# HGRN2 readout on 32-column TensorE tiles, gates computed ahead of the backward direction, and 40 unread products a layer between HGRN2 and banded attention

## The chip, the cores and the metric

One core of a Trainium2 chip runs the whole program: a two-layer hybrid diffusion backbone. TensorE (PE) does the products and the transposes, VectorE (DVE) and ScalarE (ACT) the elementwise work, GpSimd (POOL) a little, and SyncE (SP) issues the DMAs. The metric is device time in microseconds (us) of one execution.

## The reference, cut to what matters

Each layer feeds the same normalised tokens (256 of context and 1024 latent) to four groups of heads: an S5 state space model, banded attention, HGRN2 and latent attention. HGRN2 has four heads with a state of 64 x 64, runs in both directions, and is computed in chunks of 32 tokens. With f the forget gate, q the query and v the value of a token, one head of one direction does

```
S_t = diag(f_t) S_(t-1) + (1 - f_t) v_t^T       # state, 64 keys x 64 values
y_t = q_t^T S_t                                 # readout
y   = rms_norm(y_fwd + y_bwd) * g * silu(gate)
```

In chunks, y of a token is the sum of an intra part (products of the 32 tokens of its own chunk, masked by a triangle) and an inter part (its decayed query times the state that enters the chunk). Latent tokens start from the last context state; in the last layer nothing is read out for context tokens.

## The kernel before

Features lie on the partitions and tokens on the free axis. The 1280 tokens come in blocks (0, 512), (512, 512) and (1024, 256); the last is the context. HGRN2 has two passes p = 0, 1 in each layer, and a pass holds two heads (64 partitions each). In a pass, `fm` computes a dense product of a block with 128 columns of the input projection (tiles `psfm`, 24 products of 128x512 or 128x256, three for each of eight slices of the features, lines L509 to L511) and hands the PSUM tile on. In this order a pass takes: the queries (`query`), the three forward units, the three backward units (`unit`, called with the direction and the block), and for each block the gate and the end (`finish`). Between these calls the S5 mixer and, in layer 0, the modulation columns (`mods`; tiles `modps`, `modt`) are written a step at a time.

One unit of a 512-token block goes through the engines like this. ACT makes a softplus of the dense tile (L568 to L570), DVE the log gates (L571, L572) and their sum in each chunk (a scan, L580). ACT expands the decay to 128x1024 (L590), makes the decayed query and key (L594, L595) and the key decayed to the chunk's end (L599). PE transposes that (L604), ACT copies it (L605), PE multiplies it with v for every chunk (L613, 64 records), ACT copies the four results (L614) into the state tile `hgkv`, in which value column v and chunk c stand at v * 17 + c, so that one DVE scan (L621) runs over all chunks. Then comes the readout: PE multiplies keys with queries of 128 tokens a head (L631), DVE copies through the triangle's mask into `hgatt`, zero outside the diagonal (L633), and PE sums the intra product (L640) and the inter products (L644) in one tile `hgop`. Here the state of a chunk is the stationary operand, 64 columns at a stride of 17 floats, and 32 tokens of queries are the moving one. ACT copies `hgop` to `hgy` for the forward direction (L647), DVE adds it for the backward one (L649).

`finish` copies the gate's dense tile, makes its silu (L350 to L354, L660), squares y (L662), multiplies the square with a matrix of ones (L664, tile `hgms`), takes the inverse root on ACT (L673, L674), and ends on DVE (L666, L667) with a DMA to DRAM. Its temporary tiles `hglg` are those of the units.

The order of each engine is made at build time by a scheduler that sees tile dependencies. PSUM gives `fm` three buffers, and five of another tag (`mx`) are shared by HGRN2, S5 and the modulation. After HGRN2 comes banded attention (tiles `sws`, `swP`, L788 on), in whose PSUM pool latent attention also starts.

Of the kernel before, what the change touches and what calls it, by code (L numbers as in the profile page):

```python
# [10 lines left out]
U8 = mybir.dt.uint8  # L11
# [524 lines left out]
class HGRN:  # L536
# [12 lines left out]
    def start(self, p):  # L549
        self.p = p  # L550
        self.q, self.y, self.prev = {}, {}, [None, None]
# [6 lines left out]
    def unit(self, d, b, z):  # L558
# [6 lines left out]
        vt = self.pool.tile([128, 4, 128], F32, name="hgv", bufs=1)[:, 0:m]  # L565
        nc.sync.dma_start(vt, self.vd[:, t0 // 128:t0 // 128 + m, p * 128:p * 128 + 128])
        lg, sp, lf, cum = self.new("lg", tn, 2), self.new("sp", tn, 2), self.new("lf", tn), self.new("cum", tn)
# [31 lines left out]
        nc.scalar.activation(out=sp, in_=sp, func=AF.Exp, scale=-1.0, bias=bias)  # L599

# [6 lines left out]
        for q in range(4):  # L607
            r = slice(32 * q, 32 * q + 32)
            ps = self.ps(f"kvp{q}")[:, 0:64 * m].rearrange("p (m v) -> p m v", v=64)
            for i in range(m):  # L610
                for h in range(2):
                    hs = slice(64 * h, 64 * h + 64)
                    nc.tensor.matmul(ps[hs, i], kt[r, i, hs], vt[r, i, hs], start=True, stop=True)  # L613
# [11 lines left out]
        ats = []  # L625
        for h in range(2):
            r = slice(64 * h, 64 * h + 64)
            ps = self.ps(f"at{h}")[:, 0:tn].rearrange("p (m t) -> p m t", t=128)
            for i in range(m):
                ts = slice(i * 128, i * 128 + 128)  # L630
                nc.tensor.matmul(ps[:, i], kp[r, ts], qd[r, ts], start=True, stop=True)  # L631
            at = g.hgatt[h][d][:, 0:m]
            V.copy_predicated(at, g.hgtri[:, d].unsqueeze(1).to_broadcast([128, m, 128]), ps)  # L633
            ats.append(at)
        op = self.ps("op")[:, 0:tn]
        heads = slice(0, 64), slice(64, 128)
        for i in range(m):
            cl = [c for c in range(4 * i, 4 * i + 4) if before[c] is not None]
            for r, at in zip(heads, ats):
                nc.tensor.matmul(op[r, i * 128:i * 128 + 128], vt[:, i, r], at[:, i], start=True, stop=not cl)  # L640
            for c in cl:
                ts = slice(c * HC, c * HC + HC)
                for r in heads:
                    nc.tensor.matmul(op[r, ts], before[c][r], qd[r, ts], start=False, stop=c == cl[-1])  # L644
        if d == 0:
            self.y[b] = self.pool.tile([128, tn], F32, name=f"hgy{b}", bufs=1)
            nc.scalar.copy(self.y[b], op)  # L647
        else:
            V.tensor_tensor(out=self.y[b], in0=self.y[b], in1=op, op=OP.add)  # L649

    def finish(self, b, gg, ng, dst):
# [1494 lines left out]
```

## Time and profile before

| what | value |
|---|---|
| time, median of 3 runs | 3580.84 us (3575.26 to 3581.83) |
| profiled execution, its own time | 3594.48 us |
| its span | 3592.4 us |
| PE busy | 3374.6 us, 94% of the span |
| DVE, ACT busy | 2242.0 us (62%), 1517.0 us (42%) |
| mean granted clock of TensorE | 0.925 |
| HGRN2 with S5, layer 0 and layer 1 | 285 to 682 us, 2245 to 2512 us |

The busy times are those of one profiled execution, and its time lies 13.6 us above the median of the runs. The two HGRN2 stretches are read off the first and the last of their instructions in the timeline. Matmuls are pipelined, so that the duration of one record in the timeline is longer than the time to the next record; where records repeat, the start of the next group tells the pace. [...]

### The profile page before, as it was taken

The page shows a single profiled execution, that of the slowest core. Times are in us where ns is not written, and L with a number is a line of the kernel's source. Part 1 is how long each engine was busy: PE and PEld are TensorE (multiplying, and loading weights), DVE is VectorE, ACT ScalarE, POOL GpSimd, SP SyncE. Part 2 cuts the span into 40 slices and gives each one's busy share as a digit, 9 for nine tenths or more (in the row PEclk, how much of TensorE's full clock was granted, in tenths as well). Part 3 has the DMA queues.
Part 4 walks back from the last instruction along what each step waited for, and adds up shares of the span by engine and source line. Part 5 has one row for each costly group of instructions (what it writes and reads, how often), then busy time and mean ns, then how long its engine had stood idle before and what let it go on. Part 6 is the DMA issues. An engine that isn't in the chain of part 4 may idle for free.

```text
span 3592.4 us, 49905 instructions
## 1 busy us (share of the span) xinstructions
PE 3374.6 (94%) x18452; PEld 2564.5 (71%) x18452; DVE 2242.0 (62%) x4615; ACT 1517.0 (42%) x2804; POOL 210.5 (6%) x165
## 2 busy tenths in 40 slices
PE   7999999899999899999999999898999989999898
PEld 4876766555457777888788887776554668888786
DVE  8764454446746988555487724655566576566676
ACT  4144334334544523333354524655344553333344
POOL 0000000002320000000000000000035100000000
PEclk9998887579999899999999999887699999999999
DMA  6434353312032333222544433222010423333733
GB/s 206 156 128 154 121 168 111 97 41 70 29 116 98 108 109 115 87 93 74 203 160 117 129 105 109 78 85 60 18 45 11 155 98 122 97 106 106 246 97 109
DMA packets 251860, 389.54 MB, mean 108 GB/s; under 512 B 41648, under 2 KB 125840, under 8 KB 250848
## 3 DMA queue, kind: packets, MB, share of 16 engines
q1 hardware_dynamic: 240208, 374.69, 32.2%
q0 software_dynamic: 2192, 8.23, 0.9%
q10 hardware_dynamic: 9216, 3.44, 0.4%
q8 instruction: 145, 2.38, 0.3%
q14 instruction: 99, 0.81, 0.1%
HBM read 283.42 MB, written 102.83 MB: 108 GB/s over the span
## 4 chain that ended last, share of the span: by engine, by line
PE 81%; DVE 10%; ACT 4%; DMA 3%; issue 1%; SPq 0%; ACTq 0%; DVEq 0%
PE fpd L510 4%; PE fpd L511 4%; PE fpd L509 4%; PE fpx L509 4%; PE fpx L510 4%; PE fpx L511 4%; PE psfm L509 3%; PE psfm L511 3%; PE psfm L510 3%; PE mlo L1044 3%; PE fpw L509 2%; PE fpw L511 2%; PE fpw L510 2%; PE hgop L644 2%; PE sws L790 2%; PE pso L509 2%
## 5 line engine op out<-in xcount | busy, mean ns | idle before, releaser
L509 PE MATMUL fpd<-bhr,dhr 128*128 128x512 f32 (+1 forms) x792 | 280.5, 368 | 17.9 <-ACT bhr L515 10.3
L510 PE MATMUL fpd<-blr,dhr 128*128 128x512 f32 (+1 forms) x792 | 291.6, 370 | 2.3 <-DVE blr L518 2.3
L511 PE MATMUL fpd<-bhr,dlr 128*128 128x512 f32 (+1 forms) x792 | 289.1, 367 | 0.0
L509 PE MATMUL psfm<-Hh,wfh 128*128 128x512 f32 (+1 forms) x704 | 269.8, 383 | 1.8 <-ACT hgq L556 1.2
L511 PE MATMUL psfm<-Hh,wfl 128*128 128x512 f32 (+1 forms) x704 | 265.9, 378 | 0.0
L510 PE MATMUL psfm<-Hl,wfh 128*128 128x512 f32 (+1 forms) x704 | 264.7, 376 | 0.0
L509 PE MATMUL fpx<-Th,fh 128*128 128x512 f32 x528 | 208.3, 394 | 25.2 <-ACT fh L515 22.9
L515 ACT CAST fh<-fs 128x512 fp32r<-128x512 f32 x176 | 108.8, 621 | 239.9 <-PE fpc L510 68.8
L510 PE MATMUL fpx<-Tl,fh 128*128 128x512 f32 x528 | 207.7, 393 | 1.8 <-DVE Tl L1290 1.8
L511 PE MATMUL fpx<-Th,fl 128*128 128x512 f32 x528 | 207.3, 393 | 0.0
L515 ACT CAST fh<-fq 128x512 fp32r<-128x512 f32 x160 | 99.1, 621 | 222.1 <-issue 93.5
L509 PEld LDWEIGHTS fpd<-bhr,dhr 128*128 128x128 f32 x792 | 147.4, 190 | 42.8 <-ACT bhr L515 18.3
L518 DVE TENSOR_TENSOR fl<-fq,fh 128x512 fp32r<-128x512 f32 x160 | 109.9, 688 | 106.6 <-ACT fh L515 106.6
L510 PEld LDWEIGHTS fpd<-blr,dhr 128*128 128x128 f32 x792 | 150.0, 189 | 30.6 <-DVE blr L518 5.4
L1014 DVE TENSOR_REDUCE mlmc<-mls 128x1 f32<-128x512 f32 (+1 forms) x200 | 114.3, 590 | 88.1 <-PE mls L1013 87.6
L511 PEld LDWEIGHTS fpd<-bhr,dlr 128*128 128x128 f32 x792 | 150.0, 189 | 24.1 <-issue 0.2
L509 PEld LDWEIGHTS psfm<-Hh,wfh 128*128 128x128 f32 x704 | 137.1, 195 | 36.0 <-issue 12.3
L511 PEld LDWEIGHTS psfm<-Hh,wfl 128*128 128x128 f32 x704 | 136.6, 194 | 29.4 <-issue 9.2
L510 PEld LDWEIGHTS psfm<-Hl,wfh 128*128 128x128 f32 x704 | 137.0, 195 | 26.6 <-issue 7.4
L1040 ACT ACTIVATE mlpt<-mlst 128x512 f32<-128x512 f32 (+1 forms) x168 | 97.5, 585 | 113.9 <-PE mlst L511 107.3
L1077 POOL TENSOR_TENSOR mlac<-mlac,mlpt 128x1024 f32<-128x1024 f32 x56 | 137.5, 2455 | 116.2 <-ACT mlpt L1040 115.5
L518 DVE TENSOR_TENSOR fl<-fs,fh 128x512 fp32r<-128x512 f32 x176 | 120.8, 688 | 29.0 <-ACT fh L515 26.5
(529 smaller groups left out, 8539.1 us busy)
## 6 DMA issues: line engine op xcount, KB each, us to landing
fq<-in_w_up SPq DMA_DIRECT2D x188, 256.0 KB, 2.6
btok<-gd SPq DMA_DIRECT2D x154, 256.0 KB, 2.8
modw<-in_w_mod SPq DMA_DIRECT2D x128, 256.0 KB, 3.7
gd<-fg SPq DMA_DIRECT2D x88, 256.0 KB, 2.1
gd<-fgt SPq DMA_DIRECT2D x66, 256.0 KB, 2.1
mw<-in_w_down SPq DMA_DIRECT2D x66, 256.0 KB, 4.5
mw<-in_w_mod SPq DMA_DIRECT2D x32, 512.0 KB, 6.1
wor<-in_w_out SPq DMA_DIRECT2D x32, 512.0 KB, 3.6
```

The lines of the kernel that those rows point to most:

```text
L509: nc.tensor.matmul(ps, wh, xh, start=first and i == 0, stop=False, skip_group_check=read)
L510: nc.tensor.matmul(ps, wh, xl, start=False, stop=False, skip_group_check=read)
L511: nc.tensor.matmul(ps, wl, xh, start=False, stop=last and i == n - 1, skip_group_check=read)
L515: i = g.nc.scalar.copy(hi, src)
L518: (eng or g.nc.vector).tensor_tensor(out=lo, in0=src, in1=hi.bitcast(F32), op=OP.subtract)
L644: nc.tensor.matmul(op[r, ts], before[c][r], qd[r, ts], start=False, stop=c == cl[-1])
L790: nc.tensor.matmul(out, q[r], kl[r, c0:c1], start=False, stop=stop)
L1014: V.tensor_reduce(out=mc[:, qb, j:j + 1], in_=s, axis=AX.X, op=OP.max)
L1040: nc.scalar.activation(out=pt, in_=ps, func=AF.Exp, scale=MLA_SCALE)
L1044: nc.tensor.matmul(po[c], vt[:, b, 64 * h:64 * h + 64], pt[:, e], start=first, stop=last)
L1077: (V if h == 3 and b > 5 else nc.gpsimd).tensor_tensor(out=acc, in0=acc if b > 1 else prev, in1=pt, op=OP.add)
```

## The change

It has four parts.

1. **Readout.** Keys times queries is done for a chunk of 32 tokens alone: 32 products of 32x32 a unit (new L608) instead of 8 of 128x128. It stands ahead of the transposes, and the masked copy (L612, now 128 columns a head) ahead of the state scan. The intra product is 32 products on 32x32 tiles (L645), the inter product 32 products (L650), in which the decayed query is the stationary operand (64 x 32) and the state of the chunk, 64 columns at a stride of 17 floats, the moving one. So y comes out with tokens on the partitions, in two tiles (one a head), and `finish` transposes it back on PE (L679, tile `hgyt`, four of 128x128 for a block of 512).
2. **Order.** A new `gate` (copy, sigmoid, product into `hgsg`) is called for all blocks before the backward direction, and `finish` of a block right behind its backward unit. The plan in which the input projection's weights are loaded follows.
3. **Buffers.** `hglg` has one buffer in place of two, `hgv` two in place of one, `hgatt` becomes two small tiles a direction, the mask of the scan is bfloat16.
4. **Unread products.** 40 bfloat16 products of 128x256 (L1815, tile `run`) are written ahead of banded attention; nothing reads them. The scheduler sets them between the instructions of the last unit.

```diff
-        lg, sp, lf, cum = self.new("lg", tn, 2), self.new("sp", tn, 2), self.new("lf", tn), self.new("cum", tn)
+        lg, sp, lf, cum = self.new("lg", tn), self.new("sp", tn, 2), self.new("lf", tn), self.new("cum", tn)
...
+            for i in range(m):
+                for c in range(4):
+                    ts = slice(i * 128 + c * HC, i * 128 + c * HC + HC)
+                    for r, ps in zip(heads, pss):
+                        nc.tensor.matmul(ps[32 * c:32 * c + 32, i], kp[r, ts], qd[r, ts], start=True, stop=True)
+            at = g.hgatt[d][self.count[d] % 2]
+            self.count[d] += 1
+            for h in range(2):
+                V.copy_predicated(at[:, h, 0:m], g.hgtri[:, d].unsqueeze(1).to_broadcast([128, m, HC]), pss[h])
...
-                nc.tensor.matmul(ps[:, i], kp[r, ts], qd[r, ts], start=True, stop=True)
...
-            for r, at in zip(heads, ats):
-                nc.tensor.matmul(op[r, i * 128:i * 128 + 128], vt[:, i, r], at[:, i], start=True, stop=not cl)
-            for c in cl:
-                ts = slice(c * HC, c * HC + HC)
-                for r in heads:
-                    nc.tensor.matmul(op[r, ts], before[c][r], qd[r, ts], start=False, stop=c == cl[-1])
+            for h, r in enumerate(heads):
+                for c in range(4):
+                    k = slice(32 * c, 32 * c + 32)
+                    nc.tensor.matmul(ops[h][k, i], at[k, h, i], vt[k, i, r], start=i == 0, stop=False)
+        for c in range(n):
+            if before[c] is not None:
+                k = slice(32 * (c % 4), 32 * (c % 4) + 32)
+                for h, r in enumerate(heads):
+                    nc.tensor.matmul(ops[h][k, c // 4], qd[r, c * HC:c * HC + HC], before[c][r], start=False, stop=c == end[c % 4])
...
+        yt = self.ps("yt")[:, 0:tn]
+        for i in range(0, tn, 128):
+            nc.tensor.transpose(yt[:, i:i + 128], y[:, i:i + 128], g.ident)
+        nc.scalar.activation(out=sq, in_=yt, func=AF.Square)
...
                     for b, t0, tn, ps in fm(4 * p + 3, last):
-                        hg.finish(b, ps, g.hgng[:, l:l + 1], ysc[p][l])
+                        hg.gate(b, ps)
                         next(s5, None)
+                    for b, t0, tn, ps in fm(4 * p + 1, order=(2, 1, 0)):
+                        hg.unit(1, b, ps)
+                        next(s5, None)
+                        if not last or t0 < TL:
+                            hg.finish(b, g.hgng[:, l:l + 1], ysc[p][l])
...
+            ps = mpp.tile([128, 512], F32, name="run", tag="mdp")
+            for _ in range(40):
+                nc.tensor.matmul(ps[:, 0:256], g.identb, g.swmask.rearrange("p a b -> p (a b)"), start=True, stop=True)
```

On ACT, the last two backward units of layer 0 stood like this before: the copies of one unit's state products (L614), then already the next unit's decay (L590), whose softplus lies further ahead, and at the end three `finish` calls in a row.

```order
L614 COPY hgkv<-hgkvp_5971 128x4x64
L590 ACTIVATE hgdec<-hgcum 128x64x16
L595 ACTIVATE hgkp<-hgsp 128x512
L599 ACTIVATE hgsp<-hgsp 128x512
L1136 COPY modr<-modps 128x256 x2
L605 COPY hgkt<-hgtp 128x512
L614 COPY hgkv<-hgkvp_6129 128x4x64
```

Now, at the same place (L626 is the copy of the state products, L680, L691 and L692 are the three ACT steps of `finish`, L568 the first step of the next unit):

```order
L626 COPY hgkv<-hgkvp_6587 128x4x64
L680 ACTIVATE hglg<-hgyt 128x512
L691 ACTIVATE hglg<-hgms,eps 128x512
L692 ACTIVATE hglg<-hglg 128x512
L568 ACTIVATE hglg<-psfm 128x512
L569 ACTIVATE hglg<-hglg 128x512
L570 ACTIVATE hglg<-hglg 128x512
L590 ACTIVATE hgdec<-hgcum 128x64x16
```

The next unit's softplus moved behind the whole `finish` of the unit ahead of it.

On PE, the end of HGRN2 in layer 1 stood like this before (the last dense product, the last of four groups of readout, the two `hgms` and the first two products of banded attention):

```order
L511 MATMUL psfm<-Hh_18818,wfl 128x512
L640 MATMUL hgop<-hgatt_20418,hgv 64x128
...
L644 MATMUL hgop<-hgqd,hgkv 64x32 x8
L664 MATMUL hgms<-hglg,ones_134 128x512 x2
L788 MATMUL sws<-swo_22864,swo_22870 128x256
L790 MATMUL sws<-swkl,swo_22870 128x256
```

Now the last dense product stands ahead of the key products of the last unit but one, and a whole unit with its `finish` follows between the `run` products:

```order
L511 MATMUL psfm<-Hh_19830,wfl 128x512
L608 MATMUL hgat_23436<-hgqd,hgkp 32x32
...
L617 MATMUL hgtp<-ident,hgsp 128x128 x4
...
L682 MATMUL hgms<-hglg,ones_134 128x512
L1815 LDWEIGHTS identb
L1815 MATMUL run<-swmask,identb 128x256
...
L679 MATMUL hgyt<-ident,hgy_22915 128x128 x4
L682 MATMUL hgms<-hglg,ones_134 128x512
L805 MATMUL sws<-swo_23896,swo_23902 128x256
```

The dense products that stood between the units of the last pass moved ahead of the last two backward units. In layer 1, 24 `run` products stand ahead of the last unit's key products and 16 between its steps; in layer 0, 13 stand ahead, 25 between and 2 behind.

## Rows read from the trace of the kernel before

**Rows 1.** The page: engines' busy time, TensorE's granted clock in 40 slices, last chain.

```profile
PE 3374.6 (94%) x18452; PEld 2564.5 (71%) x18452; DVE 2242.0 (62%) x4615; ACT 1517.0 (42%) x2804; POOL 210.5 (6%) x165
...
PEclk9998887579999899999999999887699999999999
...
PE 81%; DVE 10%; ACT 4%; DMA 3%; issue 1%; SPq 0%; ACTq 0%; DVEq 0%
```

**Rows 2.** Windows: start:end, length, busy (records) by engine, granted clock, DMA share, GB/s.

```profile
280.00:690.00 410.00, 370.32 (x3100) 265.30 (x3099) 200.05 (x402) 161.37 (x317) 8.02 (x24) 0.80 0.41 127
2240.00:2512.00 272.00, 238.16 (x2127) 189.80 (x2125) 168.96 (x315) 148.50 (x275) 8.23 (x24) 0.83 0.25 77
636.80:681.90 45.10, 34.34 (x291) 21.37 (x291) 14.04 (x22) 15.60 (x26) 0.21 (x1) 0.53 0.19 58
2495.60:2511.80 16.20, 9.76 (x85) 6.12 (x85) 6.20 (x9) 5.64 (x10) 0.00 (x0) 0.62 0.09 21
698.00:768.00 70.00, 70.00 (x252) 41.88 (x251) 29.73 (x80) 21.99 (x56) 1.76 (x3) 0.54 0.14 43
2512.00:2558.00 46.00, 42.02 (x131) 24.98 (x130) 23.37 (x51) 18.48 (x41) 1.58 (x1) 0.50 0.13 37
```

**Rows 3.** Groups by line on PE: records, busy us, mean ns, idle before.

```profile
L644 PE MATMUL hgop<-hgqd,hgkv 64*64 64x32 f32 x1136 | 79.2, 295 | 0.0
L640 PE MATMUL hgop<-hgatt,hgv 128*64 128x128 f32 x288 | 53.6, 397 | 32.8 <-DVE hgatt L633 32.7
L631 PE MATMUL hgat<-hgqd,hgkp 64*128 64x128 f32 x288 | 36.0, 307 | 0.1
L613 PE MATMUL hgkvp<-hgv,hgkt 32*64 32x64 f32 x1280 | 32.3, 240 | 2.5 <-ACT hgkt L605 2.4
L604 PE MATMUL hgtp<-ident,hgsp 128*128 128x128 f32 x80 | 17.1, 333 | 8.5 <-ACT hgsp L599 8.5
L805 PE MATMUL sws<-swmask,identb 128*128 128x128 bf16 x64 | 16.2, 252 | 0.0
```

**Rows 4.** Groups by line, PE's weight loads: records, busy us, mean ns, idle before.

```profile
L644 PEld LDWEIGHTS hgop<-hgqd,hgkv 64*64 64x64 f32 x1136 | 69.9, 202 | 20.5 <-issue 19.6 <-ACT hgsp L599 0.5 <-ACT hgkp L595 0.3
L613 PEld LDWEIGHTS hgkvp<-hgv,hgkt 32*64 32x64 f32 x1280 | 28.8, 146 | 12.0 <-ACT hgkt L605 7.6 <-issue 1.4 <-ACT hglg L569 0.7
```

**Rows 5.** Timeline of PE, end of layer 1: start, us, line, records [idle before].

```profile
2495.24 0.39 PE L511 MATMUL psfm<-Hh,wfl 128*128 128x512 f32 x1
2497.25 0.95 PE L640 MATMUL hgop<-hgatt,hgv 128*64 128x128 f32 x4 [1.62 <-DVE hgatt L633]
2498.12 1.09 PE L644 MATMUL hgop<-hgqd,hgkv 64*64 64x32 f32 x16
2511.83 1.20 PE L788 MATMUL sws<-swo,swo 128*128 128x256 f32 x1
```

**Rows 6.** Timeline of PE, end of layer 0.

```profile
636.41 0.40 PE L511 MATMUL psfm<-Hh,wfl 128*128 128x512 f32 x1
655.06 2.59 PE L613 MATMUL hgkvp<-hgv,hgkt 32*64 32x64 f32 x64 [0.68 <-ACT hgkt L605]
...
667.11 1.11 PE L644 MATMUL hgop<-hgqd,hgkv 64*64 64x32 f32 x16
681.95 1.20 PE L788 MATMUL sws<-swo,swo 128*128 128x256 f32 x1
692.23 3.22 PE L1134 MATMUL modps<-mw,scp 128*32 128x512 f32 x8 [1.60 <-DMA mw<-in_w_mod]
```

**Rows 7.** Timeline of ACT and DVE, steps of units and of an end, 512 tokens.

```profile
638.20 1.99 ACT L590 ACTIVATE hgdec<-hgcum 128x1024 f32<-128x1024 f32 x1 [2.56 <-DVE hgkv L621]
656.22 2.09 ACT L614 COPY hgkv<-hgkvp 128x256 f32<-128x256 f32 x4 [1.21 <-PE hgkvp L613]
658.40 2.42 DVE L621 TENSOR_TENSOR_SCAN hgkv<-hgdec,hgkv 128x1088 f32<-128x1088 f32 x1 [7.74 <-ACT hgkv L614]
682.97 0.69 ACT L673 ACTIVATE hglg<-hgms,eps 128x512 f32<-128x512 f32 x1 [0.98 <-PE hgms L664]
```

More of the change, by code (lines that the diff above doesn't have):

```diff
@@ L610, in unit @@
             for i in range(m):
-                for h in range(2):
-                    hs = slice(64 * h, 64 * h + 64)
+                for hs in heads:
                     nc.tensor.matmul(ps[hs, i], kt[r, i, hs], vt[r, i, hs], start=True, stop=True)
@@ L635, in unit @@
[L635 to L644 removed]
+        ops = [self.ps(f"op{h}")[:, 0:64 * m].rearrange("p (m v) -> p m v", v=64) for h in range(2)]
@@ new lines, in unit @@
+        end = [max(c for c in range(j, n, 4) if before[c] is not None) for j in range(4)]
+        for i in range(m):
+            for h, r in enumerate(heads):
[7 more added lines that the diff above has]
+                    nc.tensor.matmul(ops[h][k, c // 4], qd[r, c * HC:c * HC + HC], before[c][r], start=False, stop=c == end[c % 4])
@@ L645, in unit @@
         if d == 0:
             self.y[b] = self.pool.tile([128, tn], F32, name=f"hgy{b}", bufs=1)
[L647 to L651, printed above, removed]
+        y = self.y[b].rearrange("p (m h v) -> p h m v", h=2, v=64)
+        for h in range(2):
+            if d == 0:
+                nc.scalar.copy(y[:, h], ops[h])
+            else:
+                V.tensor_tensor(out=y[:, h], in0=y[:, h], in1=ops[h], op=OP.add)
@@ L653, in finish, with gate @@
+    def gate(self, b, gg):
+        g, nc = self.g, self.g.nc
+        tn = BLOCKS[b][1]
+        gc, self.sg[b] = self.new("lf", tn), self.pool.tile([128, tn], F32, name=f"hgsg{b}", bufs=1)
+        nc.scalar.copy(gc, gg)
+        sigmoid(g, self.sg[b], gc, self.new("lg", tn))
+        nc.vector.tensor_tensor(out=self.sg[b], in0=self.sg[b], in1=gc, op=OP.mult)
+    def finish(self, b, ng, dst):
         g, nc = self.g, self.g.nc
@@ L1770, in hybrid_kernel @@
                         next(s5, None)
-                    for d in range(2):
-                        for b, t0, tn, ps in fm(4 * p + d, order=((2, 0, 1), (2, 1, 0))[d]):
-                            hg.unit(d, b, ps)
+                    for b, t0, tn, ps in fm(4 * p):
+                        hg.unit(0, b, ps)
+                        next(s5, None)
+                        if last and t0 == 512:
                             next(s5, None)
-                            if last and d == 0 and t0 == 512:
-                                next(s5, None)
                     for b, t0, tn, ps in fm(4 * p + 3, last):
-                        hg.finish(b, ps, g.hgng[:, l:l + 1], ysc[p][l])
+                        hg.gate(b, ps)
                         next(s5, None)
+                    for b, t0, tn, ps in fm(4 * p + 1, order=(2, 1, 0)):
+                        hg.unit(1, b, ps)
+                        next(s5, None)
+                        if not last or t0 < TL:
+                            hg.finish(b, g.hgng[:, l:l + 1], ysc[p][l])
                 for _ in (*s5, *fill):
```

46 lines of the change are left out of this document (17 added, 29 removed).

## The prediction

> **What bounds the kernel now.** I read the page first: PE is busy 94% of the span and makes 81% of the chain that ended last, while the clock row dips at slices 4 to 8 and 26 to 29 of 40, about 90 us each [rows 1]. Those are the places of HGRN2 and the start of banded attention, so the windows come next. They show two kinds of stretch. In the body of HGRN2, PE is busy 370.3 of 410 us in layer 0 and 238.2 of 272 us in layer 1 at a granted clock of 0.80 and 0.83 [rows 2]: dense products fill the waits of the recurrence, so a PE product taken away there is time won. From the last dense product to the first product of banded attention, PE has little to put into its waits: 45.1 us in layer 0, of which 34.3 are work, and 16.2 us in layer 1, of which 9.8 are work [rows 2, 5, 6]. There the time is the latency of a chain through PE, ACT and DVE. So the change has to be priced twice, as work and as latency. A third kind lies behind: banded attention runs its first 70 us and 46 us at 0.50 to 0.54, though PE is busy 100% and 91% [rows 2].
>
> **The readout, as work.** Before, it takes 36.0 + 53.6 + 79.2 = 168.8 us [rows 3]. The chip records each of these float32 products twice (a unit of a 512-token block has 8, 8 and 32, the timeline 16, 16 and 64). There are 18 units' worth of readout: 288 / 16. The new code has three times 32 products a unit, less those of the chunks without an entering state: 1152 records for the keys, 1152 for the intra part, 1136 for the inter part.
>
> No row shows a 32x32 tile. The nearest is the state product L613, 32x64 tiles in runs of 64: 32.3 us / 1280 = 25 ns a record [rows 3], 40 ns in the run at half clock (2.59 us for 64) [rows 6]. The new tiles are smaller, and contiguous on both sides for keys and intra part, so I take 25 ns: 29 us each. The inter part is unlike L613, since the state with its stride of 17 floats is now streamed. The only rows that touch this state are L644's: 69 ns a record (1.11 us for 16), and the same 1.09 to 1.11 us at either clock [rows 5, 6], with weight loads of 69.9 / 1136 = 62 ns where the contiguous ones of L613 cost 28.8 / 1280 = 22 ns [rows 4]. That speaks for a price on the stride, not on arithmetic. A streamed state could cost 25 ns a record (28 us), if the stride hurts weight loads alone, or 138 ns (157 us), if one record has to read the 64 columns twice. I take 45 ns, 51 us, between L613 and L644, because eight tiles can stream beside each other where L644 had two. Sum: 29 + 29 + 51 = 109 us, a saving of **60 us**; the ends are 83 us saved and 46 us lost (29 + 29 + 157 = 215).
>
> [...]
>
> **The transposes back.** 36 of 128x128 (20 in layer 0, 16 in layer 1), at L604's 17.1 / 80 = 214 ns [rows 3]: **+8 us** of PE. The smaller masked copies and the two half-width copies or adds of y lie on DVE and ACT, beside PE, in the body; I count nothing. In a last unit they are in the chain below.
>
> **The masked copy.** PE waited 32.8 us for it ahead of L640 [rows 3], because it stood behind the scan of 2.42 us [rows 7]. It now stands ahead of the scan, and its 32-column products far ahead. But the inter products still need the scan, which needs the last copy of the state products. What is late next is the scan itself, hidden by the intra products (some 1 us) and S5 or modulation steps that the order sets there. I take a third back: **-12 us**, from 0 to -20.
>
> **The order, as latency.** With one `hglg` buffer, the next unit's first ACT step waits until `finish` of the unit ahead has let the buffer go; the listings show it right behind that `finish`'s two root steps. Queued behind it on ACT are the unit's decay, keys and copies, and all of PE's and DVE's steps of that unit wait for them. So backward units now run one after another. The length of one with its `finish`, for 512 tokens: decay 1.99, copies 2.09, scan 2.42 [rows 7], 6.5 us; some 15 further steps of ACT and DVE on 512 columns at about 0.69 (as L673) [rows 7], 10.4 us; PE's transposes, the part of its state products ahead of the copies, inter part, transposes back and `hgms`, 6 us; and handoffs, some 15 at 0.2, 3 us. Together 26 us, an estimate.
>
> In the body, dense products, S5 and modulation fill that chain: the order puts 24 to 63 dense products between backward units of the first pass. For the change of passes, where S5 runs thin, I add 4 us in each layer, **+8 us**. In the tail there is little left. Layer 0: the rest of the context unit (8 us), a unit (26), and a unit up to its `hgms` (24) make 58 us. PE's own steps in it, at half clock, come to about 24 (2.5 units at 9.6: key products 1, transposes both ways 1.8, state products 2.6, intra and inter 2.4, `hgms` 2), so 34 us are idle against 45.1 - 34.3 = 10.8 before: **+23 us**. Layer 1: the rest of a unit from its key products on (18) and a unit (27, with two ACT steps that only layer 1 has), 45 us, PE's part 19, idle 26 against 6.4: **+20 us**. Working with idle time alone keeps the readout's saving from being counted twice.
>
> **The unread products.** 80 of 256 columns. Nearest is the mask product L805, also bfloat16: 16.2 us / 64 = 253 ns for 128 columns, with its own latency in it [rows 3]; twice that for 256 columns is 40 us, the columns alone at the two clock levels 8.5 or 17 us. The order has nearly all of them in waits of the last units, which are idle anyway, so they cost what stands at the end of a wait: **+2 us**, up to +10. If that cover were gone, 8.5 to 17 us would come on.
>
> **The clock.** In the tails it is 0.53 and 0.62 [rows 2]: once the dense products end, PE works mostly at the lower level. In the body, less of PE's time goes to small products; at 0.80 [rows 2] that is worth perhaps **-10 us** (0 to -20). Whether the unread products hold the higher level through the tail and into banded attention is the largest open gain. If its first 70 and 46 us ran at the higher level from the start, and two fifths of their time are bound by the clock (my guess, with the rest in waits for softmax steps), that gives -28 and -18, -46 us. Against it: they fill 10 to 20 us of some 60 idle ones; and behind the tail come waits that the change leaves alone, for the first softmax and for a weight DMA (1.60 us ahead of L1134 at 692 us) [rows 6]. PE at 100% busy from 698 us on did not lift the clock for 70 us.
>
> **Sum.** Against the profiled execution of 3594.48 us: -60 + 8 - 12 + 8 + 23 + 20 + 2 - 10 = -21 us, 3573.5. The profiled one lies 13.6 us above the median of the runs; the same -21 on 3580.84 gives **3560 us**.
>
> **Rivals.**
>
> *The clock holds.* The unread products keep the higher level into banded attention: -21 - 46 = -67, 3514 us. For it: it is full PE work with no dependency, 24 of them in one run ahead of layer 1's last unit. Against it: the idle time just told. Chance 0.22.
>
> *Streaming the strided columns is dear.* Place: the inter products L650, 1136 records in each of which the state is the moving operand. At more than 45 + 21 / 1.136 = 63 ns a record the whole gain is gone; at L644's 69 ns the sum is +6 us, at 100 ns 62 us come on, 3622 us. For it: L644's pace does not follow the clock and its weight loads are three times L613's [rows 4 to 6]. Against it: more tiles beside each other, and fewer columns loaded. Chance 0.15. [...]
>
> *The serial chain is not covered in the first pass either.* Each layer has about 2.5 and 2 backward units of 26 us there, some 117 us; if a third of it stands idle, +39 in place of +8, which gives +10, 3591 us; with waits of the stores and of S5 behind it, more. Chance 0.08.
>
> *The change does not do what it says.* The readout is faster by its 60 us, but the tails take it back in full (idle 40 and 35 us and no gain in clock or mask wait): within 7 us of 3581. Chance 0.13.
>
> **How the numbers follow.** Forecast 3560 (3536 to 3574) 0.42, clock 0.22, even 0.13, dear stream 0.15, open chain 0.08. What a measurement of this kernel can tell from no change is about 0.2%, 7 us. Faster: 0.42 + 0.22 = 0.64; within: 0.13; slower: 0.23. The range has to leave out no more than 2 in 10: down to 3505, a little below the clock rival with some of the readout's better end, and up to 3615, which takes in half of the dear-stream case. The likeliest case alone spans 3536 to 3574.
>
> **What would show it.** Right, if the three new readout groups sum to 90 to 125 us; if the stretch from the last dense product to `sws` is 53 to 63 us in layer 0 and 40 to 50 in layer 1, with the next unit's L568 starting behind L692; if the wait ahead of the intra product is gone and one ahead of L650 for the scan appears. The clock rival shows as 1.00 in the first 40 us of banded attention. A mean of more than 63 ns for an L650 record, or an idle share of PE above 10% in the first pass's backward units, would make the forecast wrong on the slow side; records at 17 ns and a covered tail, on the fast side.

## The result, and the profile after

The changed kernel takes 3523.01 us (median, 3521.56 to 3524.69) against 3578.05 us for the kernel before: a ratio of 0.9857, 95% interval 0.9831 to 0.9883, 55 us faster. The forecast was 3560 us in a range of 3505 to 3615 us, so the direction and the range held, and the size was 2.6 times what the sum had given. Executions of one kernel spread by 3 to 43 us here, so single profiles are compared by stretch below and not by their span. The kernel before was timed again beside each group of runs, with medians from 3574.17 to 3584.00 us; each ratio below is against the kernel before in the same group, and times of different groups (changed kernel; e1 to e4; e5 to e8; e9 and e10; e11) compare only to about 10 us.

The page after, in the lines that answer to [rows 1]:

```profile
PE 3255.9 (92%) x20296; PEld 2474.1 (70%) x20296; DVE 2230.0 (63%) x4625; ACT 1517.8 (43%) x2814; POOL 209.5 (6%) x165
...
PEclk9999987699999999999999999987799999999999
...
PE 75%; DVE 12%; ACT 5%; DMA 4%; issue 2%; SPq 0%; ACTq 0%; DVEq 0%
```

PE is busy 118.7 us less, though it has 1,844 more records, and its share of the last chain falls from 81% to 75% in favour of DVE, ACT and DMA. The windows that answer to [rows 2] (start:end, length, busy and records of PE, PEld, DVE, ACT, POOL, granted clock, DMA share, GB/s): for each layer the body up to the last dense product, the tail up to the first `sws`, and the start of banded attention.

```profile
281.00:590.50 309.50, 278.72 (x3377) 193.12 (x3376) 162.91 (x360) 133.70 (x275) 6.72 (x20) 0.91 0.51 156
590.50:656.30 65.80, 36.15 (x726) 24.82 (x725) 25.08 (x38) 23.06 (x38) 1.46 (x4) 0.58 0.19 49
656.30:726.00 69.70, 66.08 (x300) 38.51 (x297) 38.86 (x98) 29.93 (x69) 2.16 (x4) 0.76 0.29 86
2196.00:2404.80 208.80, 176.40 (x2356) 141.22 (x2354) 142.14 (x290) 126.45 (x246) 3.94 (x15) 0.89 0.27 83
2404.80:2452.00 47.20, 25.06 (x573) 18.45 (x573) 20.36 (x26) 21.45 (x30) 4.32 (x9) 0.68 0.28 73
2452.00:2498.00 46.00, 42.03 (x131) 25.16 (x129) 22.78 (x50) 18.14 (x40) 1.58 (x1) 0.50 0.13 34
```

The two bodies of the kernel before, in the same bounds:

```profile
281.00:636.80 355.80, 328.96 (x2789) 239.96 (x2788) 179.90 (x368) 140.55 (x280) 7.81 (x23) 0.84 0.44 137
2242.00:2495.60 253.60, 226.21 (x2025) 181.48 (x2023) 161.20 (x305) 141.18 (x262) 8.23 (x24) 0.84 0.26 80
```

The traces before and after hold two values of the granted clock, 0.50 and 1.00; they are the lower and the higher level below, and a window's figure is the mean over it. The bodies are shorter and run at a higher clock (0.91 and 0.89 against 0.84), the tails are longer (65.8 us against 45.1, 47.2 against 16.2) with 29.7 and 22.1 us of PE idle in them, and banded attention starts at 0.76 in layer 0 and still at 0.50 in layer 1. Over body and tail of both layers, PE's idle time goes from 71.4 to 115.0 us, and its busy time from 599.3 to 516.3 us. The new groups on PE (records, busy us, mean ns, idle before) answer to [rows 3]:

```profile
L645 PE MATMUL hgop<-hgv,hgatt 32*32 32x64 f32 x1152 | 25.1, 241 | 1.5 <-ACT hgkv L626 0.7 <-DVE hgatt L612 0.7
L650 PE MATMUL hgop<-hgkv,hgqd 64*32 64x64 f32 x1136 | 21.5, 292 | 33.2 <-DVE hgkv L633 33.2
...
L1815 PE MATMUL run<-swmask,identb 128*128 128x256 bf16 x80 | 14.6, 337 | 0.0
L608 PE MATMUL hgat<-hgqd,hgkp 64*32 64x32 f32 x1152 | 14.5, 218 | 41.5 <-DVE hgqd L596 41.5
...
L679 PE MATMUL hgyt<-ident,hgy 128*128 128x128 f32 x36 | 8.3, 369 | 4.1 <-DVE hgy L658 4.1
```

The readout's three parts take 14.5 + 25.1 + 21.5 = 61.1 us in place of 168.8, and two new waits have come up: 33.2 us for the state scan ahead of the inter products, and 41.5 us for the decayed queries ahead of the key products.

This table gives the stretches of every kernel's profile, in us, between the starts of the first and last records of its timeline that bound them: body (first softplus to last dense product), tail (to the first `sws`), banded (to the last `sws`), for layer 0 (L0) and layer 1 (L1), and latent attention of layer 1. What is not shown adds up to 2461 to 2470 us in every kernel.

| kernel | body L0 | tail L0 | banded L0 | body L1 | tail L1 | banded L1 | latent L1 |
|---|---|---|---|---|---|---|---|
| before | 355.6 | 45.5 | 169.8 | 252.7 | 16.6 | 130.3 | 160.6 |
| after | 309.0 | 66.2 | 146.6 | 208.5 | 47.6 | 123.3 | 155.9 |
| e1_no_run | 306.1 | 64.9 | 168.0 | 210.1 | 49.5 | 123.2 | 155.9 |
| e2_readout_only | 320.1 | 11.7 | 164.3 | 221.2 | 2.8 | 122.8 | 155.9 |
| e3_run_only | 356.4 | 47.9 | 165.4 | 252.2 | 16.5 | 121.4 | 155.9 |
| e4_square_elsewhere | 302.7 | 45.1 | 151.4 | 200.7 | 35.2 | 130.4 | 159.0 |
| e5_readout_run | 313.1 | 13.7 | 157.3 | 221.1 | 6.4 | 123.0 | 155.8 |
| e6_finish_late | 302.5 | 38.0 | 161.4 | 200.4 | 33.8 | 127.0 | 160.4 |
| e7_one_buffer | 320.2 | 17.2 | 168.7 | 220.3 | 6.0 | 130.1 | 162.0 |
| e8_run_160 | 305.1 | 79.5 | 148.5 | 209.7 | 59.1 | 136.3 | 155.8 |
| e9_contiguous_moving | 308.9 | 61.1 | 150.4 | 208.4 | 48.1 | 130.3 | 160.7 |
| e10_contiguous_weights | 342.1 | 45.4 | 151.8 | 245.2 | 15.6 | 118.8 | 155.8 |
| e11_run_layer0 | 304.3 | 63.8 | 145.4 | 209.7 | 47.5 | 123.6 | 160.1 |

From before to after, body and tail together give 25.9 us in layer 0 and 13.2 us in layer 1, banded attention gives 23.2 us in layer 0. The 7.0 us of banded and 4.7 us of latent attention in layer 1 are not shown to be an effect of the change: e3_run_only has them too, with the HGRN2 code of before, and the banded stretch of layer 1, whose own products no kernel changes, lies between 118.8 and 136.3 us over all profiles.

### The profile page after: what moved, and what is told of

Its sections match the earlier page's. It is cut to its first block, busy times and chain, and to the rows that moved or that the text cites. A ratio compares the mean times of both kernels' runs of the same rounds, so it can differ in the third digit from the quotient of the medians.

```text
span 3520.6 us, 53595 instructions
## 1 busy us (share of the span) xinstructions
PE 3255.9 (92%) x20296; PEld 2474.1 (70%) x20296; DVE 2230.0 (63%) x4625; ACT 1517.8 (43%) x2814; POOL 209.5 (6%) x165
## 4 chain that ended last, share of the span: by engine, by line
PE 75%; DVE 12%; ACT 5%; DMA 4%; issue 2%; SPq 0%; ACTq 0%; DVEq 0%
PE fpd L510 5%; PE fpd L511 4%; PE fpd L509 4%; PE fpx L511 4%; PE fpx L510 4%; PE fpx L509 4%; PE psfm L509 3%; PE psfm L510 3%; PE mlo L1061 3%; PE psfm L511 3%; PE fpw L511 2%; PE fpw L509 2%; PE fpw L510 2%; PE pso L509 2%; PE pso L511 2%; PE pso L510 2%
## 5 line engine op out<-in xcount | busy, mean ns | idle before, releaser
L509 PE MATMUL fpx<-Th,fh 128*128 128x512 f32 x528 | 208.5, 395 | 25.5 <-ACT fh L515 22.9
L511 PEld LDWEIGHTS fpd<-bhr,dlr 128*128 128x128 f32 x792 | 150.4, 190 | 24.3 <-issue 0.2
L509 PEld LDWEIGHTS psfm<-Hh,wfh 128*128 128x128 f32 x704 | 135.7, 193 | 38.8 <-issue 13.5
```

Source lines behind the costliest of these rows:

```text
L509: nc.tensor.matmul(ps, wh, xh, start=first and i == 0, stop=False, skip_group_check=read)
L511: nc.tensor.matmul(ps, wl, xh, start=False, stop=last and i == n - 1, skip_group_check=read)
```

## The experiments

**Each part alone or left out.** The first takes the unread products out of the changed kernel.

```diff
-            for _ in range(40):
-                nc.tensor.matmul(ps[:, 0:256], g.identb, g.swmask.rearrange("p a b -> p (a b)"), start=True, stop=True)
```

> The changed kernel without the 40 unread products a layer. Theory A (the unread products bring the clock back early in banded attention of layer 0, 662 to 687 us at 0.50 instead of some 85 us): those 60 us run at 0.50 again, the stretch from the first to the last sws of layer 0 grows from 147 to 165 to 172 us, and the time from 3523 to 3543 to 3550 us. Theory B (the clock there comes back early for another reason, such as less small work ahead of it): stretch 145 to 150 us, time 3518 to 3526 us.

Measured: 3541.12 us (ratio 0.989, 0.9839 to 0.9941), 18 us over the changed kernel and 2 us under theory A's range, with the banded stretch of layer 0 at 168.0 us, as theory A had it. Every execution of e1 (3538.05 us at least) is slower than every one of the changed kernel (3524.69 us at most), but they stand in different groups, and the intervals of the two ratios overlap. In layer 1 the stretch is 123.2 us without the products and 123.3 with them: there they do nothing that shows.

The second keeps the new readout and undoes order, unread products and the single `hglg` buffer.

```diff
-        lg, sp, lf, cum = self.new("lg", tn), self.new("sp", tn, 2), self.new("lf", tn), self.new("cum", tn)
+        lg, sp, lf, cum = self.new("lg", tn, 2), self.new("sp", tn, 2), self.new("lf", tn), self.new("cum", tn)
...
-                    for b, t0, tn, ps in fm(4 * p + 3, last):
-                        hg.gate(b, ps)
...
+                    for d in range(2):
+                        for b, t0, tn, ps in fm(4 * p + d, order=((2, 0, 1), (2, 1, 0))[d]):
+                            hg.unit(d, b, ps)
...
+                    for b, t0, tn, ps in fm(4 * p + 3, last):
+                        hg.gate(b, ps)
+                        hg.finish(b, g.hgng[:, l:l + 1], ysc[p][l])
```

> The new readout and its transposes back, with the gates at the end as before, finish after the backward direction, two hglg buffers, and no unread products. Theory A (the readout saves about 100 us of PE work and the new order gives some 55 us back in the tails): faster than the changed kernel, 3485 to 3505 us; tails (last dense product to first sws) 35 to 45 us in layer 0 and 12 to 20 us in layer 1. Theory B (the order is part of the gain, since the mask copy and the scan are late next without it): 3530 to 3555 us.

Measured: 3460.07 us (ratio 0.9647, 0.9597 to 0.9697). It is 63 us faster than the changed kernel, beyond theory A's range in the time as in the tails (11.7 and 2.8 us): the new readout gives 115 us, and the new order takes 3541 - 3460 = 81 us of it back. Where they go is seen in body and tail of layer 0 and of layer 1, first of e1_no_run:

```profile
278.70:584.80 306.10, 274.73 (x3374) 188.91 (x3372) 162.78 (x359) 133.13 (x275) 6.75 (x20) 0.93 0.51 158
584.80:649.70 64.90, 31.06 (x689) 21.10 (x687) 25.37 (x39) 23.07 (x38) 1.46 (x4) 0.53 0.18 50
2213.00:2423.10 210.10, 179.77 (x2356) 142.23 (x2354) 141.85 (x290) 127.19 (x246) 3.94 (x15) 0.89 0.27 81
2423.10:2472.60 49.50, 20.97 (x534) 15.49 (x533) 20.65 (x26) 21.76 (x30) 4.32 (x9) 0.55 0.27 76
```

and then of e2_readout_only:

```profile
281.60:601.70 320.10, 287.17 (x4040) 206.28 (x4039) 181.73 (x388) 145.91 (x297) 8.22 (x24) 0.91 0.52 159
601.70:613.40 11.70, 6.59 (x23) 3.86 (x21) 3.89 (x7) 7.97 (x15) 0.00 (x0) 0.65 0.07 24
2174.50:2395.70 221.20, 186.07 (x2881) 149.77 (x2880) 157.75 (x301) 143.02 (x268) 8.25 (x24) 0.92 0.30 91
2395.70:2398.50 2.80, 1.42 (x9) 0.83 (x7) 0.98 (x2) 2.29 (x5) 0.00 (x0) 1.00 0.25 94
```

Length less PE's busy time is 124.1 us of idle in the four stretches of e1 and 74.5 us in those of e2, 50 us more. PE's busy time is 506.5 us against 481.3, 25 us more for the same instructions: in the tails they run at 0.53 and 0.55, in e2 nearly all of them stand in bodies at 0.91 and 0.92. That the clock is the cause is read from this and from single groups (the same 20 `hgms` products take 16.2 us in e1 and 11.9 us in e2); no run sets the clock alone. Together that is 75 of the 81 us; the other 6 us are not located. e2's own tails hold only the transposes back and the last `hgms` steps, because the gates' dense products stand between the units and behind the last one. In the kernel before, the scheduler set the last of them ahead of the last two units' inter products [rows 6], so the edit of the readout moved the cover too. Its sum is not changed by that: PE's idle time over body and tail is 71.4 us before and 74.5 us in e2.

The third adds the unread products alone to the kernel before.

```diff
+            ps = mpp.tile([128, 512], F32, name="run", tag="mdp")
+            for _ in range(40):
+                nc.tensor.matmul(ps[:, 0:256], g.identb, g.swmask.rearrange("p a b -> p (a b)"), start=True, stop=True)
```

> The kernel before with only the 40 unread products a layer added. Theory A (they lift the clock in banded attention wherever they stand): 3550 to 3565 us, and a first stretch at 0.50 in banded attention of layer 0 that is shorter by 20 us or more. Theory B (they are too few, or stand in the wrong place, for the clock): 3576 to 3590 us, the stretch as long as before.

Measured: 3568.16 us against 3575.57 (ratio 0.9966, 0.9941 to 0.9992): 7 us faster, between the theories. Its banded stretch of layer 0, 165.4 us, is 4.4 us shorter than before.

The fourth takes `finish` off the shared buffer and has it use `hgkt`, which a unit needs only later.

```diff
-        sq = self.new("lg", tn)
+        sq = self.new("kt", tn)
```

> The changed kernel with the square of finish in the tile hgkt, so that a unit's softplus no longer waits for the finish ahead of it. Theory A (the single hglg buffer makes the units serial): about 5 us of softplus and log gates leave the chain of each unit in the tails, 8 to 20 us in all, 3503 to 3515 us, tails of 50 to 60 us and 38 to 44 us where they are 66 and 48. Theory B (the state scan and what follows it are serial anyway, and the softplus was not late): within 4 us of 3523.

Measured: 3485.67 us (ratio 0.9717, 0.9666 to 0.9767), 37 us faster than the changed kernel, twice what theory A gave. The tails are 45.1 and 35.2 us where they were 66.2 and 47.6, and the bodies also shorten, by 6.3 and 7.8 us: the chain had not been covered there either. Body and tail together are 47.6 us shorter; banded attention, which varies between profiles (118.8 to 136.3 us in layer 1 over the table), is 4.8 and 7.1 us longer in this profile. How the one buffer makes the units serial is seen on ACT in the changed kernel (timeline: start, us, line, tile [idle before]):

```profile
609.21 0.60 ACT L568 ACTIVATE hglg<-psfm 128x512 f32<-128x512 f32 x1 [0.55 <-DVE hgy L684]
...
629.27 0.60 ACT L680 ACTIVATE hglg<-hgyt 128x512 f32<-128x512 f32 x1 [5.76 <-PE hgyt L679]
632.03 0.69 ACT L691 ACTIVATE hglg<-hgms,eps 128x512 f32<-128x512 f32 x1 [2.16 <-PE hgms L682]
632.75 0.63 ACT L692 ACTIVATE hglg<-hglg 128x512 f32<-128x512 f32 x1
634.19 0.60 ACT L568 ACTIVATE hglg<-psfm 128x512 f32<-128x512 f32 x1 [0.82 <-DVE hgy L684]
```

A unit's first step (L568) starts when `finish` of the one ahead has let the buffer go, by DVE's L684. From one L568 to the next is 25.0 us. In e4 a wait of this kind is left, now ahead of a later step of the unit, its copy into `hgkt`:

```profile
617.01 0.58 ACT L618 COPY hgkt<-hgtp 128x512 f32<-128x512 f32 x1 [0.87 <-DVE hgy L684]
```

In the body of the changed kernel the chain is covered in part only. From the context unit's last copies of state products to the first L568 behind the last `finish`, which takes in the two 512-token backward units of the first pass, PE is idle for 9.5 of 63.7 us in layer 0 and 9.6 of 56.1 us in layer 1, 15% and 17%:

```profile
411.40:475.10 63.70, 54.20 (x807) 37.77 (x807) 30.77 (x56) 31.12 (x58) 0.86 (x4) 0.89 0.31 96
2277.00:2333.10 56.10, 46.47 (x682) 36.13 (x680) 23.13 (x34) 28.69 (x51) 1.45 (x5) 0.88 0.20 65
```

**What in the order costs.** The next kernel is e2_readout_only with the unread products (the diff is that of e3_run_only).

> The new readout in the order of before (as e2_readout_only) with the 40 unread products a layer. Theory A (they bring the clock back early in banded attention of layer 0 if they stand just ahead of it): 3435 to 3452 us, the stretch from the first to the last sws of layer 0 at 142 to 150 us. Theory B (without idle tails they only add their own 80 products at 0.1 to 0.2 us and do not lift the clock): 3458 to 3478 us, the stretch at 160 to 168 us.

Measured: 3458.55 us (ratio 0.9681, 0.9637 to 0.9726), the same as e2: theory B by the time. The stretch is 157.3 us, between the theories, and the tails are 2.0 and 3.6 us longer.

Then the changed kernel without unread products, with `finish` behind all three backward units:

```diff
-                        if not last or t0 < TL:
-                            hg.finish(b, g.hgng[:, l:l + 1], ysc[p][l])
+                    for b in ((2, 1, 0) if not last else (1, 0)):
+                        hg.finish(b, g.hgng[:, l:l + 1], ysc[p][l])
```

> The changed kernel without unread products, gates still ahead of the backward direction, but the three finish calls of a pass behind its three backward units. Theory A (finish between the units makes them serial through the one hglg buffer): tails shorter than those of e1_no_run (65 and 50 us) by 15 us or more each, 3495 to 3515 us where e1_no_run has 3541. Theory B (the tails are long because the gates' dense products no longer stand in them): tails within 8 us of e1_no_run, 3530 to 3545 us.

Measured: 3484.98 us (ratio 0.9753, 0.9696 to 0.9809), 56 us faster than e1_no_run and beyond theory A's range; tails 38.0 and 33.8 us. So of the order's 81 us, 56 come from `finish` standing between units that share its buffer; body and tail show 55.9 us of it, and e4, which takes only the buffer away, gave 47.6 us by the same stretches against the changed kernel. The other 25 come with the rest, the gates' dense products ahead of the backward direction, which leave the tails without cover, and the one buffer (next run); body and tail show 18.9 us of them. The wait of the key products, PE's first step in a unit, tells the same: e1, e2, e4 and e6 in turn, beside the 41.5 us of the changed kernel.

```profile
L608 PE MATMUL hgat<-hgqd,hgkp 64*32 64x32 f32 x1152 | 14.3, 215 | 46.2 <-DVE hgqd L596 46.2
L608 PE MATMUL hgat<-hgqd,hgkp 64*32 64x32 f32 x1152 | 14.7, 206 | 13.9 <-DVE hgqd L596 12.8 <-ACT hgkp L595 1.1
L608 PE MATMUL hgat<-hgqd,hgkp 64*32 64x32 f32 x1152 | 14.3, 209 | 10.6 <-DVE hgqd L596 7.9 <-ACT hgkp L595 2.7
L608 PE MATMUL hgat<-hgqd,hgkp 64*32 64x32 f32 x1152 | 14.9, 216 | 11.6 <-DVE hgqd L596 10.0 <-ACT hgkp L595 1.6
```

Then e2_readout_only with one buffer:

```diff
-        lg, sp, lf, cum = self.new("lg", tn, 2), self.new("sp", tn, 2), self.new("lf", tn), self.new("cum", tn)
+        lg, sp, lf, cum = self.new("lg", tn), self.new("sp", tn, 2), self.new("lf", tn), self.new("cum", tn)
```

> The new readout in the order of before (as e2_readout_only) with one hglg buffer in place of two. Theory A (one buffer hurts only where finish stands between units): 3460 to 3472 us. Rival (the buffer itself costs, in the body too, where forward units and gates share it): 3480 us or more.

Measured: 3466.6 us (ratio 0.9715, 0.9658 to 0.9772), theory A. One buffer in itself costs 6.5 us by the medians, which is within the spread of the executions; one buffer with `finish` between the units costs 56 us.

**Can more unread products hold the clock?** The changed kernel with 160 in place of 40 a layer.

> The changed kernel with 160 unread products a layer in place of 40. Theory A (they fill the idle time of the last units and hold the higher clock there and at the start of banded attention): 3490 to 3515 us, the 25 us at 0.50 after the first sws of layer 0 and the 51 us of layer 1 gone or halved. Theory B (the clock falls in the softmax waits behind them whatever stands ahead): 3523 to 3540 us, since the further 240 products cost 0.1 us each wherever they exceed the idle time.

Measured: 3572.48 us (ratio 0.998, 0.9951 to 1.001), 49 us slower than with 40, and above what theory B allowed. In each layer, most of the additional products were set in one row (122 and 109 records) behind the last `hgms`, ahead of the first `sws` (timeline of PE, the windows right behind it, and the group):

```profile
653.45 13.48 PE L1815 MATMUL run<-swmask,identb 128*128 128x256 bf16 x122
...
666.70:672.00 5.30, 3.72 (x21) 1.71 (x18) 1.61 (x4) 1.17 (x2) 0.00 (x0) 1.00 0.51 145
672.00:713.00 41.00, 40.23 (x133) 24.96 (x134) 18.28 (x49) 14.98 (x40) 1.37 (x2) 0.50 0.12 33
...
L1815 PE MATMUL run<-swmask,identb 128*128 128x256 bf16 x320 | 42.8, 296 | 0.0
```

In layer 0 the clock is at the higher level during the row (a product takes 13.48 / 122 = 0.110 us, and 0.109 at 1.00 and 0.213 at 0.50 in the changed kernel, from start to start) and for the first 5 us of banded attention (1.00), then at the lower one for 41 us (0.50). The tails grow by 13.3 and 11.5 us, and banded attention of layer 1 by 13.0 us. The changed kernel shows the same fall with 40 products:

```profile
656.30:662.00 5.70, 3.00 (x14) 1.69 (x11) 3.88 (x8) 3.32 (x6) 0.00 (x0) 0.83 0.32 80
662.00:687.00 25.00, 24.08 (x75) 13.08 (x75) 13.72 (x30) 10.54 (x23) 0.96 (x1) 0.50 0.51 155
687.00:726.00 39.00, 39.00 (x213) 23.74 (x213) 21.27 (x61) 16.07 (x42) 1.20 (x3) 0.91 0.14 43
```

In its first 5.7 us PE is busy 3.0 us (of the idle time, 1.92 us are a wait for the first softmax, L830), and then the clock is down, with 40 products ahead as with 160. So theory A falls.

**Where the unread products help.** The changed kernel with 40 of them in layer 0 alone.

```diff
-            for _ in range(40):
+            for _ in range(40 * (1 - l)):
```

> The changed kernel with the 40 unread products in layer 0 only. Theory A (all that they give lies in layer 0, where the clock came back 31 us after the first sws in place of 82): 3519 to 3527 us, the stretch from the first to the last sws of layer 0 at 145 to 152 us. Rival (the place where the clock comes back is chance of one execution, and the products give little): 3532 to 3545 us, the stretch at 160 us or more.

Measured: 3533.81 us (ratio 0.989, 0.9871 to 0.991), the rival by the time; the profiled execution has a stretch of 145.4 us, theory A's, but it is the fastest of six that spread from 3523.8 to 3541.8 us. Without any products, e10_contiguous_weights below also has a stretch of 151.8 us. So how much of the stretch the products decide, and how much varies between executions, is not settled. By the times, 40 a layer gave 18 us in one arrangement (e1), 7 in another (e3) and none that shows in a third (e5), 40 in layer 0 alone gave 7 (e11 against e1), and 160 a layer cost 31 us (e8 against e1). All but e3's compare different groups of runs. What decides it stays open.

**The stride of the state.** Two kernels read 64 contiguous floats of the same tile where they read 64 at a stride of 17 (the inter part of the output is left out in both: other values are multiplied; instructions and waits are the same). First the changed kernel, with the state as the moving operand.

```diff
-        before = [kv[:, :, c + d] for c in range(n)]
+        before = [kvf[:, (c + d) * 64:(c + d) * 64 + 64] for c in range(n)]
```

> The changed kernel with the inter products reading 64 contiguous floats of the state tile where they read 64 at a stride of 17 (other values: the inter part of the output is not the reference's; same instructions, same waits). Theory A (a strided moving operand costs nothing on tiles of this size): L650 stays at 18 to 20 ns a record, time within 5 us of 3523. Theory B (the stride has a price, hidden in the 18.6 ns beside the 13.8 ns of the key products): 13 to 15 ns a record, 5 to 8 us faster.

Then the same edit in the kernel before, where the state is the stationary operand.

> The kernel before with the inter products loading 64 contiguous floats of the state tile as weights where they load 64 at a stride of 17 (other values: the inter part of the output is not the reference's; same instructions, same waits). Theory A (the 69 ns a record of the old inter products are the price of loading strided weights): L644 falls to 22 to 35 ns a record, its sum from 79 to 25 to 40 us, and the time by 35 to 50 us. Theory B (they are the price of 64x64 tiles on one diagonal, that is of the shape): 60 to 70 ns a record, time within 8 us of the kernel before.

Timeline of PE: with the stride, after, at 0.50 and at 1.00,

```profile
626.08 1.19 PE L650 MATMUL hgop<-hgkv,hgqd 64*32 64x64 f32 x64 [1.38 <-DVE hgkv L633]
...
2447.13 1.14 PE L650 MATMUL hgop<-hgkv,hgqd 64*32 64x64 f32 x64 [2.26 <-DVE hgkv L633]
```

contiguous and moving, at 0.50 and at 1.00,

```profile
618.04 1.18 PE L650 MATMUL hgop<-hgkv,hgqd 64*32 64x64 f32 x64 [1.38 <-DVE hgkv L633]
643.12 0.86 PE L650 MATMUL hgop<-hgkv,hgqd 64*32 64x64 f32 x64 [2.25 <-DVE hgkv L633]
```

and contiguous as weights in the kernel before, at 1.00 and at 0.50:

```profile
413.42 0.66 PE L644 MATMUL hgop<-hgqd,hgkv 64*64 64x32 f32 x16
...
441.28 1.07 PE L644 MATMUL hgop<-hgqd,hgkv 64*64 64x32 f32 x16
```

A run's time divided by its records, with the end of its last record in it, is 13.4 ns contiguous and 17.8 ns strided at the higher level for the streamed state, 18.4 and 18.6 ns at the lower. As weights it is 41 ns contiguous and 68 ns strided (1.09 us for 16 at 2498.12 us, granted clock 1.00 [rows 5]) at the higher level, 67 and 69 ns (1.11 us at 667.11 us, 0.50 [rows 6]) at the lower. So both theories on the weights are half right: the shape alone costs 41 to 67 ns, and the stride adds 27 ns where the clock is high. In the sums, the moving operand's stride costs 21.5 - 18.1 = 3.4 us, that of the weights 79.2 - 68.3 = 10.9 us, with each execution's own mix of clock levels in it.

The times were 3523.78 us for e9 (ratio 0.984, 0.98 to 0.9881), the same as after: by the pace of the moving operand theory B of e9 holds, by the time theory A. They were 3552.86 us for e10 (ratio 0.9917, 0.988 to 0.9953), 31 us under before and between its theories. The bodies show 13.5 + 7.5 us of that. The profiles of e10 and of before can't place the rest: they lie 15 us under and 14 us above their medians, and 29.5 us of the difference between them stand in banded attention, which the edit doesn't touch.

## Why the prediction was right in direction and range, and wrong in size

**The range held in part by luck.** 3523 us lies outside the likeliest case (3536 to 3574 us), between it and the clock rival's 3514, and the sum came near because terms that were far off had opposite signs; they follow one by one.

**The two kinds of stretch: right.** The body pays work and the tail pays latency. e2_readout_only, which leaves PE's idle time as it was (74.5 us against 71.4), gained 115 us: PE's busy time falls by 118.0 us. Its readout takes 60.2 us, 108.6 less, its transposes add 6.9, and the other 16 us are the same other products in less time, at the higher clock of its bodies (0.91 and 0.92 against 0.84).

**The readout: the term that failed most.** Forecast 109 us, measured 61.1. The step was "I take 25 ns": L613's mean over both clock levels, for tiles with 64 moving columns, was carried to tiles of 32x32 as if it were a floor. Measured were 14.5 / 1152 = 12.6 ns for the keys, 25.1 / 1152 = 21.8 ns for the intra part and 21.5 / 1136 = 18.9 ns for the inter part. All three lie below the 25 ns that I had taken as the lower bound. For the inter part I took 45 ns between L613 and L644; the choice rested on reading L644's 69 ns as a price of the stride that would go along with the operand. e9 and e10 show that the shape makes most of it and that a moving operand pays 4.4 ns for the stride at the higher clock level. The rival of the dear stream is thereby out. In these runs a stride of 17 floats has a price, 4.4 ns a record moving and 27 ns as weights at a granted clock of 1.00, and under 3 ns at 0.50; no run has another stride, so what makes the price is not shown. That products on separate tiles stream beside each other, the ground for 45 ns, shows in the pace: 64 contiguous columns take 13.4 ns a record on the 64x32 tiles (e9), where they would take 27 ns at the pace of L1815's 256 columns on a 128x128 tile, 109 ns from start to start (both at 1.00). Single records of L650 start eight within 51 ns and the next eight from 102 ns on (2447.13 us), those of L644 in pairs, 111 to 134 ns from one pair to the next (2498.12 us of the kernel before).

L613's 25 ns mixes both clock levels; the key products undercut it in a run at one of them. 64 records, 32 products on separate tiles with 32 moving columns, take 0.76 us at granted clock 1.00 with the end of the last one in it, 11.9 ns a record and 23.8 ns a product:

```profile
355.31 0.76 PE L608 MATMUL hgat<-hgqd,hgkp 64*32 64x32 f32 x64
```

**The transposes back: right.** 8 us forecast, 8.3 measured.

**The masked copy: the reason right, the size wrong.** The wait of 32.8 us ahead of L640 [rows 3] is gone, and the scan, named as late next, took its place with 33.2 us ahead of L650. Nothing came back of the 12 us that I had counted: the idle time of e2, which has this edit, is 3.1 us above that of before. The cover by intra products and S5 was smaller than the scan.

**The order as latency: the mechanism right, its price too low.** A unit's chain was put at 26 us and measures 25.0. The 0.2 us a handoff in it was my estimate and stood in no row: in the tail of layer 0 after, an engine that waited for another one starts 0.05 us behind that one's end (mean of 47). The tails were put at 58 and 45 us and are 65.8 and 47.2, with 29.7 and 22.1 us idle, forecast 34 and 26. The order was charged 23 + 20 + 8 = 51 us of idle time over the kernel before; the changed kernel has 34.6 us more in its tails and 9.0 more in its bodies, and e1 against e2 shows 50. The sign named for an open chain, PE idle for over 10% in the first pass's backward units, came true (15% and 17%), but the rival didn't: the bodies' idle time rose by the 9.0 us just told, near the +8 of the sum and far from the rival's +39. What the sum left out is that work moved from the body to the tail also runs there at the lower clock, 25 us by the reading above, so the order costs 81 us (the other 6 us are not located). I had put the clock in as a gain of 10 us for the body alone. And I weighed this order against the order of before as one piece: that `finish` between the units is two thirds of its price, and that the price hangs on the shared buffer, only e4 and e6 showed.

**The unread products: the forecast of +2 us probably wrong in sign, the clock rival not as described.** They are 14.6 us of PE, nearly all in idle time, as said, and lie between the 8.5 and 17 us told for their columns: at 0.109 and 0.213 us from start to start, 80 take 8.7 us at 1.00 and 17.0 us at 0.50. They add little: body and tail of both layers are 631.3 us with them and 630.6 without (e1). The clock rival, at 0.22, gave 46 us in both layers; 18 us came by the medians, by the profiles in layer 0 alone, and e11 leaves open how much of it is theirs. Its sign, 1.00 in the first 40 us of banded attention, did not show: the clock was 0.50 for 25 us of them in layer 0, and 0.50 over the first 46 us in layer 1.

**The sum by runs:** -115 (e2 against before), +81 (e1 against e2) and -18 (after against e1) make -52 us; that they meet the 55 us measured follows from taking the differences in a chain, and confirms nothing. Beside them stand the forecasts: -60 + 8 - 12 - 10 = -74 for what e2 has, +51 for the order, +2 for the unread products, -21 together. So the readout with its clock was 41 us better, the order 30 us worse and the unread products up to 20 us better than forecast, and the errors partly hid each other.

**Slips in the working.** The rival of no change does not add up by its own terms: -60 + 8 + 8 + 29 + 29 + 2 is +16 us, not within 7. PE's steps of a unit sum to 9.8 and not 9.6 us, and the clock row dips in slices 4 to 9. None of them moves the forecast time by more than 1 us.

The faster kernel is the new readout in the old order: 3460.07 us (e2) or, with the unread products, 3458.55 us (e5), 3.5% and 3.2% under the kernel before in their comparisons, and 63 us under the changed one.

## What to carry to other kernels

Price a move of work twice: by the idle time that it opens where it came to stand, and by the clock that it will run at there (here 50 and 25 us). A temporary buffer shared by the end of one iteration and the start of the next cost 7 us at most here while the ends stood behind all iterations, and 48 to 56 us once they stood between; look up whose buffer the first step of an iteration takes. Small products on separate tiles ran far faster here than the nearest larger tiles suggested (12.6 against 25 ns a record), so measure one run of them before they are priced.

## What the runs showed of the hardware that was not expected

- Products on tiles of 64x32 and 32x32 pace at 12.6 to 21.8 ns a record (25 to 44 ns a float32 product), where the inter and intra parts on 64x64 and 128x64 tiles took 70 and 186 ns a record (79.2 / 1136, 53.6 / 288 [rows 3]; the latter with 128 moving columns).
- A stride of 17 floats shows at a granted clock of 1.00 almost alone: 68 against 41 ns as weights, 17.8 against 13.4 ns moving. At 0.50 the figures are 69 against 67 and 18.6 against 18.4.
- In e8, full PE work of 13.5 us just ahead of banded attention of layer 0 left the higher level in place for 5.3 us; then it went for 41 us, at a PE busy share of 98%.
